# The Fourier branch's linear map on half the positions, gated there, in an encoder block on one core

## The chip, the cores and the metric

The kernel runs on one core of a Trainium2 chip. A core has a matrix engine (TensorE, PE in the profile, with its weight loads as PEld), a vector engine (VectorE, DVE), an activation engine (ScalarE, ACT), a general one (GpSimd, POOL), a queue that mostly issues transfers (SyncE, SP), and 16 DMA engines. They run side by side, each in its own order of instructions, and wait for each other by semaphores. The metric is the device time of one execution in microseconds (us).

## What is computed

One layer of an encoder on two sequences with shared weights: 1024 positions ("sample") and 256 ("prompt"), each with 16 learned meta positions ahead, width 1024. The part that matters here:

```python
z = rms_norm(x) @ w_in                  # q | k | v | f (512) | gate logits attn (1024) | gate logits four (1024)
a  = bidirectional_gqa(q, k, v) @ w_attn_o
fo = fourier_mix(f) @ w_four_o          # real part of the 2-D DFT over positions and 128 group channels
merged = sigmoid(z_ga) * a + sigmoid(z_gf) * fo
x = x + merged @ w_out                  # then a SwiGLU with a second norm, and a final norm
```

The real part of such a transform has a symmetry: with E (cosine in both directions) and O (sine in both), the value at position l and channel k is E - O or E + O, and at the mirrored position L - l the sign in front of O changes. So E and O need to be known only for positions up to L/2, and channels up to 64.

## The kernel before

All is in float32; a product is made of three matmuls on float32r parts, high x high, high x low and low x high (`three`, the lines L218 to L220, so that most matmuls carry these lines whatever they compute). Parts are made by a cast on ACT (high) and a subtraction on DVE or POOL (low). SBUF is 48 equal slots, given out in the order of the program, the longest free first.

The 1280 output positions are three chunks of 512, 512 (sample) and 256 columns (prompt). The stages, in order:

- A: norms, transposed activations `hT[c]` of each chunk, and the Fourier channels f.
- B and C: `fourier`, `q_pass`, `kv_pass`. `fourier` makes E and O: for the prompt all 256 positions unfolded, for the sample 520 positions, copied a second time mirrored with ACT. They go to DRAM (`f_d`, by chunk). `weave` puts steps of a gate generator between the steps of these passes, a share of their cost. `gate_gen([0], ...)` makes the 16 units (128 columns each) of gate logits of chunk 0: weights loaded, split, 24 matmuls, the result copied by ACT and stored in DRAM.
- D: `attention`, a unit is a query tile (128) and a key head, four query heads to a unit. A step is one query head: scores S (six matmuls for the sample, L898, into one buffer of three banks), maximum on DVE (L903), exponential on ACT (L910), scaling by the reciprocal sum on DVE (L915). Between them run the transposes (L832) of the unit before, their casts (L834) and low parts (L835), and the products with the values (L852, L853). The order on PE, ACT and DVE is the program's. Gate units of chunks 1 and 2 fill PE: at two points of each step a `Filler` gets credit in nanoseconds and issues steps of the generator for it; what these need of other engines is put into `later` and released at the second point (the "slack" point).
- E: `merge([0])`, then `merge([1, 2])`: for each of 8 units of 128 output columns load the weights (`w_m`: 4 k tiles of attention, 4 of Fourier; `w_mb`, whose sums with the Fourier half DVE makes at L992 and L993), split them (ACT, POOL), load both gates, sigmoid of both on ACT, for each chunk 4 k tiles of matmuls for the attention and 4 for the Fourier half, then two products with the gates (L1036, L1037), a sum (L1038) and the parts for the output projection. `load_af` brings attention and Fourier rows of a chunk and splits them. Then `w_out`.
- F: the SwiGLU, from 940 us on.

The functions that the change touches, and what calls them:

Of the kernel before, what the change touches and what calls it, by code (L numbers as in the profile page):

```python
# [9 lines left out]
F32 = mybir.dt.float32  # L10
# [26 lines left out]
# pairs of token tiles of the SwiGLU's products: the first three with 384 columns, the others with 256  # L37
# [18 lines left out]
SLOT = 1056  # L56
N_SLOTS = 27
# [58 lines left out]
class Slot:  # L116
# [32 lines left out]

class Filler:  # L150
    """Steps of a generator on demand."""

    def __init__(self, gen):
        self.gen, self.debt, self.live = gen, 0.0, True

    def __call__(self, cost):
        self.debt += cost
        while self.live and self.debt > 0:
            try:
                self.debt -= next(self.gen)  # L160
            except StopIteration:
                self.live = False
# [11 lines left out]
class Kernel:  # L174
    def __init__(self, tc, nc, a, o, pools):
# [18 lines left out]
        self.f_d = [self.dram.tile([512, n], F32, name=f"f_d{i}") for i, n in enumerate(CH_N)]  # L194

# [17 lines left out]
    def three(self, out, pairs, first=True, last=True):  # L213
        """out += hi.hi + hi.lo + lo.hi over pairs of ((stationary hi, lo), (moving hi, lo))."""
# [7 lines left out]
    def rstd(self, ss, n, scale, eps, name):  # L222
        """(ss * scale + eps) ** -0.5 for n sums a partition."""
# [7 lines left out]
    def norm(self, x, out, g, rows=P, name=""):  # L231
        """out = x * rsqrt(mean(x^2) + eps) (* g) along the columns."""
# [16 lines left out]
    # hT of chunk c: k pairs a slot (c0, c1), three k a slot (c2 with the meta tokens behind)  # L249
# [22 lines left out]
    def transpose_pair(self, hs, t, off, ps, name, tag="tr"):  # L272
        """Two token tiles (slots, 1024 columns) into hT columns off .. off+256."""
# [12 lines left out]
    def gained(self, t, ks, lo, hi, pt):  # L286
        """hT columns lo .. hi of some k tiles from the transposed rows, times the gains of their features."""
# [134 lines left out]

    FILL = {"s": 640, "p": 400, "end": 640, "drain": 900}

    def gate_gen(self, chunks, lo_engine):
        """Gate logits of the chunks; while there is a self.later, what is not for TensorE is put into it."""
        nc, a, sl = self.nc, self.a, self.sl
        order = list(range(16))
# [55 lines left out]

    def fourier(self, ps):
        nc, a, sl = self.nc, self.a, self.sl
        # even and odd parts over positions n <-> L - n
# [26 lines left out]
        # channels: U[n, k] for every n tile, cos from the even part, sin from the odd part  # L514
# [34 lines left out]
        for j, m in enumerate((P, 9)):  # L549
            nc.gpsimd.dma_start(tp[j][:m, :1024], a["pos_p"][j, :m])  # L550
# [25 lines left out]
        def store(kind, p, st, dst, lo, hi, c):  # L576
            """Rows of the (E0, E1, O0, O1) tiles; row 0 of each group's odd tile is k = 64."""
            d = dst[:]
            if kind == "e":
                nc.sync.dma_start(d[p * P : (p + 1) * P, :], st[:, lo:hi])  # L580
            elif kind == "o":
                for r in (0, 64):
                    b = 256 + p * P + r
                    nc.sync.dma_start(d[b + 1 : b + 64, :], st[r + 1 : r + 64, lo:hi])
            else:
                nc.sync.dma_start(d[256:512, :].rearrange("(g r) t -> g r t", g=4)[:, 0, :], st[:4, lo:hi])

        # prompt: positions 16.. unfolded
        ms = [P, 9]
        for kind, p in kinds:  # L590
            rows = 4 if kind == "4" else P
            pf = ps.tile([P, 512], F32, tag="mm", name=f"fp{kind}{p}")
            tb = 512 if kind == "o" else 0
            self.three(
                pf[:rows, :256],
                [
                    (u_of(kind, p, up, j, m), (tp[j][:m, tb : tb + 256], tp[j][:m, tb + 256 : tb + 512]))
# [4 lines left out]
            nc.vector.tensor_copy(st[:rows, :256], pf[:rows, :256])  # L602
            store(kind, p, st, self.f_d[2], 0, 256, 2)
# [3 lines left out]
        # sample: positions l = 1..520, the others mirrored  # L607
# [9 lines left out]
        for i, (kind, p) in enumerate(kinds):  # L617
# [5 lines left out]
            for half in range(2):  # L623
# [9 lines left out]
                sgn = -1.0 if kind == "o" else 1.0  # L633
                if half == 0:
                    nc.vector.tensor_copy(st[:rows, 0:245], pf[:rows, 15:260])
                    nc.scalar.mul(st[:rows, 764:1024], pf[:rows, 259::-1], sgn)
                else:
                    nc.vector.tensor_copy(st[:rows, 245:505], pf[:rows, 0:260])
                    nc.scalar.mul(st[:rows, 505:764], pf[:rows, 258::-1], sgn)
                yield 1650  # L640
            for c in range(2):
                store(kind, p, st, self.f_d[c], c * 512, (c + 1) * 512, c)
# [57 lines left out]
    def kv_pass(self, ps):  # L700
# [3 lines left out]
        # kT[seq][head][version]: columns are keys, the meta keys behind the tokens  # L704
# [94 lines left out]

    def attention(self, ps, tiles, tag_s, tag_v):  # L800
        """Scores and softmax of a unit (a query tile, a key head) run between the second products of the
        unit before it; the order is the one of the program."""
# [12 lines left out]
        class Second:  # L815
            """P^T and its product with the values, a key tile at a time."""
# [53 lines left out]
        def turns(k):  # L870
            """The k-th of the two parts of a step's share of the waiting key tiles."""
# [9 lines left out]
        for i, (t, g) in enumerate(units):  # L881
# [55 lines left out]

    def load_af(self, c):
        """a^T (4 k tiles) and Fourier (4 k tiles) of chunk c, 1024 columns a slot."""
# [29 lines left out]
    def merge(self, chunks, then):  # L969
# [35 lines left out]
        if 0 not in chunks:  # L1005
            for c in chunks:
                run_all(self.load_af(c))
# [716 lines left out]
```

## Time and profile before

| | |
|---|---|
| median of 3 runs | 1741.12 us (1739.78 to 1742.13) |
| profiled execution, first to last instruction | 1737.8 us |
| PE busy | 1697.8 us, 9917 matmuls |
| DVE / ACT / POOL busy | 1140.9 / 720.6 / 239.6 us |
| granted PE clock | 0.997 |
| moved by DMA | 212 MB, 122 GB/s over the span |

The profile lists for each engine the time in which it had an instruction under way. Matmuls overlap (the next starts before the last has left the array), so PE can be "busy" all the time and still do more or less work in it; the distance from start to start is what a matmul costs in a dense row. Groups are named by line, engine, operation and by the program's names of what is written and read; behind the bar stand busy time, mean duration in ns and the idle time before them with what ended it.

### The profile page before, as it was taken

Reading aid. Unit: us, or ns where it says so; the run is one execution under the profiler, and the core shown is the slowest. Engines: PE = TensorE matmul, PEld = TensorE weight load, DVE = VectorE, ACT = ScalarE, POOL = GpSimd, SP = SyncE. Lnnn points to the kernel's source line nnn. Section 1 sums busy time; section 2 is a strip of 40 time slices with the busy share of each in tenths; the row PEclk is TensorE's granted clock in tenths of the full one; section 3 lists DMA queues with packets and bytes.
Section 4 is the critical chain, followed back from the end, with each engine's and each line's share of the span. In section 5 each row is a group of like instructions: output and inputs, shape, how many; then the busy total and the mean of one; then the engine's idle time right before and its main releaser. Section 6 shows DMA issues by size and latency. Waiting matters only on the chain.

```text
span 1737.8 us, 25952 instructions
## 1 busy us (share of the span) xinstructions
PE 1697.8 (98%) x9917; PEld 1511.1 (87%) x9917; DVE 1140.9 (66%) x2084; ACT 720.6 (41%) x1391; POOL 239.6 (14%) x239
## 2 busy tenths in 40 slices
PE   7999999999999999999999999999999999999997
PEld 6888879878888888788879999999999998888886
DVE  5424544568777776963379766676666668765685
ACT  6323333456666666531355322222222234444444
POOL 3001333210100103423343000000000000000002
PEclk9999999999999999999999999999999999999999
DMA  5144331322222229735451222222232237553434
GB/s 190 63 149 162 116 116 55 122 74 67 70 61 59 61 79 352 250 119 170 145 182 64 85 82 95 90 96 89 94 98 84 71 126 255 198 182 101 159 97 153
DMA packets 100292, 212.06 MB, mean 122 GB/s; under 512 B 10373, under 2 KB 46877, under 8 KB 100168
## 3 DMA queue, kind: packets, MB, share of 16 engines
q1 hardware_dynamic: 90952, 192.98, 33.2%
q10 hardware_dynamic: 7824, 12.53, 2.0%
q0 software_dynamic: 1392, 4.90, 0.9%
q8 instruction: 78, 1.28, 0.3%
q14 instruction: 46, 0.38, 0.1%
HBM read 151.05 MB, written 59.31 MB: 121 GB/s over the span
## 4 chain that ended last, share of the span: by engine, by line
PE 67%; DVE 7%; DMA 3%; issue 3%; ACT 1%; POOL 1%; SPq 0%; POOLq 0%; DVEq 0%; ACTq 0%
PE i L218 9%; PE i L220 9%; PE i L219 9%; PE o L220 5%; PE o L219 5%; PE o L218 5%; PE S L898 4%; PE pt L832 4%; PE g L218 2%; PE pv L852 2%; PE g L219 2%; PE g L220 2%; PE pv L853 2%; PE wo L220 2%; PE wo L219 2%
## 5 line engine op out<-in xcount | busy, mean ns | idle before, releaser
L1227 ACT CAST w<-wi 128x512 fp32r<-128x512 f32 x168 | 104.0, 621 | 274.0 <-PE i L220 218.0
L218 PE MATMUL i<-A,w 128*128 128x384 f32 x616 | 208.4, 338 | 3.0 <-ACT w L1227 2.6
L220 PE MATMUL i<-A,w 128*128 128x384 f32 x616 | 208.1, 338 | 2.3 <-POOL w L1229 2.3
L219 PE MATMUL i<-A,w 128*128 128x384 f32 x616 | 207.9, 338 | 0.0
L218 PE MATMUL i<-Ah,w 128*128 128x256 f32 x616 | 173.0, 281 | 1.6 <-DVE sc L1283 1.5
L220 PE MATMUL i<-Ah,w 128*128 128x256 f32 x616 | 173.2, 281 | 0.0
L219 PE MATMUL i<-Al,w 128*128 128x256 f32 x616 | 172.9, 281 | 0.0
L834 ACT CAST pT<-pt 128x512 fp32r<-128x512 f32 x156 | 90.7, 582 | 97.1 <-PE pt L832 94.3
L835 DVE TENSOR_TENSOR pT<-pt,pT 128x512 fp32r<-128x512 f32 x156 | 106.9, 686 | 34.2 <-ACT pT L834 33.0
L1229 DVE TENSOR_TENSOR w<-wi,w 128x512 fp32r<-128x512 f32 x154 | 105.3, 685 | 28.7 <-ACT w L1227 28.3
L903 DVE TENSOR_REDUCE sm<-S 128x1 f32<-128x1040 f32 (+1 forms) x80 | 86.5, 1082 | 50.7 <-PE S L898 47.4
L218 PEld LDWEIGHTS i<-A,w 128*128 128x128 f32 x616 | 116.5, 189 | 3.6 <-ACT w L1227 2.9
L220 PEld LDWEIGHTS i<-A,w 128*128 128x128 f32 x616 | 116.4, 189 | 3.2 <-POOL w L1229 3.2
L218 PEld LDWEIGHTS i<-Ah,w 128*128 128x128 f32 x616 | 116.0, 188 | 2.2 <-DVE sc L1283 1.7
L219 PEld LDWEIGHTS i<-A,w 128*128 128x128 f32 x616 | 116.3, 189 | 0.0
L219 PEld LDWEIGHTS i<-Al,w 128*128 128x128 f32 x616 | 116.2, 189 | 0.0
L220 PEld LDWEIGHTS i<-Ah,w 128*128 128x128 f32 x616 | 116.0, 188 | 0.0
L227 POOL TENSOR_SCALAR fin0r<-fin0ss 128x1 f32<-128x1 f32 x1 | 0.8, 788 | 755.8 <-ACT X L235 755.8
L910 ACT ACTIVATE p<-S,sm 128x1040 f32<-128x1040 f32 (+1 forms) x80 | 80.2, 1003 | 33.6 <-DVE sm L903 27.0
L832 PE MATMUL pt<-ident,p 128*128 128x128 f32 (+1 forms) x624 | 93.4, 272 | 0.0
L220 PE MATMUL o<-wfo,act 128*128 128x512 f32 (+1 forms) x212 | 82.1, 388 | 2.1 <-DVE act L1361 2.1
L219 PE MATMUL o<-wfo,act 128*128 128x512 f32 (+1 forms) x212 | 81.9, 386 | 0.0
(745 smaller groups left out, 4475.9 us busy)
## 6 DMA issues: line engine op xcount, KB each, us to landing
wi<-w_fi SPq DMA_DIRECT2D x48, 512.0 KB
wg<-w_g SPq DMA_DIRECT2D x32, 512.0 KB
act_d<-sc SPq DMA_DIRECT2D x77, 192.0 KB
act<-act_d SPq DMA_DIRECT2D x37, 320.0 KB
wfo<-w_fo SPq DMA_DIRECT2D x21, 512.0 KB
X<-act_d SPq DMA_DIRECT2D x31, 320.0 KB
act_d<-sc SPq DMA_DIRECT2D x77, 128.0 KB
gate<-gs ACTq DMA_DIRECT2D x32, 256.0 KB
```

The source lines that it names most:

```text
L218: mm(out, sh, mh, start=first and i == 0, stop=False)
L219: mm(out, sh, ml, start=False, stop=False)
L220: mm(out, slo, mh, start=False, stop=last and i == n - 1)
L832: nc.tensor.transpose(pt[:rows, h * P : (h + 1) * P], me.ps4[h][:, col : col + rows], self.ident[:])
L834: nc.scalar.copy(pT[:rows, :512], pt[:rows, :])
L835: nc.vector.tensor_tensor(pT[:rows, 512:1024], pt[:rows, :], f32(pT[:rows, :512]), op=ALU.subtract)
L852: nc.tensor.matmul(me.pv[:], vst, pT[:rows, :512], start=j == 0, stop=False)
L898: nc.tensor.matmul(S[:, base + lo : base + hi], hq, self.kT[seq][g][v][:, lo:hi], start=v == 0, stop=v == 1)
L903: nc.vector.tensor_reduce(nb, S[:, base : base + L], axis=AX.X, op=ALU.max, negate=True)
L910: self.last_exp = nc.scalar.activation(p, S[:, base : base + L], AF.Exp, bias=nb, accum_out=total)
L1227: nc.scalar.copy(w[:, :512], src)
L1229: eng.tensor_tensor(w[:, 512:1024], src, f32(w[:, :512]), op=ALU.subtract)
```

## The change

1. `fourier` computes E and O only for positions 1 to 520 of the sample and 1 to 136 of the prompt, side by side in one table of 656 columns in DRAM; the k = 64 rows have a place of their own. The mirrored copies go.
2. The gate logits 8 to 15 (of the Fourier branch) are made for all three chunks in stages B and C, and their sigmoid is taken there before they are stored; logits 0 to 7 of chunk 0 come first in the same filler, with a share of 1.1 instead of 0.6. The attention's filler has logits 0 to 7 of chunks 1 and 2 and then a new generator, `fourier_out`; its credit is 480 and 300 ns a point instead of 640 and 400.
3. `fourier_out` applies `w_four_o` to E and O (two halves of 328 positions, two accumulators each), forms sum and difference on POOL (the second in reversed order), multiplies by the gates on POOL and stores the gated term (`fo_d`) in the order of output positions.
4. `merge` has 4 k tiles instead of 8. It loads one gate and the gated term, and keeps the split weights of the first merge (chunk 0) for the second; the low parts of these weights are made by DVE, not POOL.

The diff without the comments that it drops:

```diff
-    FILL = {"s": 640, "p": 400, "end": 640, "drain": 900}
+    FILL = {"s": 480, "p": 300, "end": 640, "drain": 900}
...
+    def __call__(self, cost, later=None):
         self.debt += cost
+        if self.held and later:
+            return
+        self.held = False
...
-            nc.scalar.copy(st[:, :n], pg[:, :n])
+            if u < 8:
+                nc.scalar.copy(st[:, :n], pg[:, :n])
+            else:
+                nc.scalar.activation(st[:, :n], pg[:, :n], AF.Sigmoid)
...
+    def fourier_out(self):
+        nc, a, sl = self.nc, self.a, self.sl
+        self.free_hT(self.hT[1])
+        self.free_hT(self.hT[2])
...
+        def need(i):
+            w = raws.pop(i)
+            vec = nc.vector.tensor_tensor
+            vec(w[:, :256], w[:, :256], w[:, 512:768], op=ALU.add)
+            vec(w[:, 256:512], w[:, 768:1024], w[:, 256:512], op=ALU.subtract)
+            u = units[i] = sl.get("wmf2", F32R)
+            nc.scalar.copy(u[:, :512], w[:, :512])
+            vec(u[:, 512:1024], w[:, :512], f32(u[:, :512]), op=ALU.subtract)
...
+        def part(r):
+            nc.scalar.copy(h[:, :NL], r[:, :NL])
+            nc.gpsimd.tensor_tensor(l[:, :NL], r[:, :NL], f32(h[:, :NL]), op=ALU.subtract)
...
+        def tail(r, t, n, lo):
+            for b in (0, 32, 64):
+                nc.scalar.copy(t[b : b + 4, :n], r[b : b + 4, :n])
+            x = slice(lo, lo + 4)
+            nc.gpsimd.tensor_tensor(t[x, :n], r[x, :n], f32(t[x, :n]), op=ALU.subtract)
...
+        do(lambda: need(0))
+        for r, t, _, n, lo in tails:
+            do(lambda r=r, t=t, n=n, lo=lo: tail(r, t, n, lo))
+        for r in raw:
+            do(lambda r=r: part(r))
+        yield 1500
+        for i in range(8):
+            for half in range(2):
...
+                    if odd == 0:
+                        nc.tensor.matmul(
+                            pm[:, :HL], y64[:68, i * P : (i + 1) * P], x64[:68, c], start=True, stop=False
+                        )
+                    for k in range(2 * odd, 2 * odd + 2):
...
+                        self.three(pm[:, :HL], [(w, (fh[k][:, c], fl[k][:, c]))], odd == 1 and k == 2, k % 2 == 1)
+                        yield 3 * HL / 2.2
+                if half == 0:
+                    do(lambda i=i: (need(i + 1), load(i + 2), load_gates(i + 1)))
+                def out(i=i, half=half, pp=pp):
+                    nc.scalar.copy(st[:, :HL], pp[0][:, :HL])
+                    nc.scalar.copy(st[:, 512 : 512 + HL], pp[1][:, :HL])
...
+                    for l, n, L, b, t0 in spans:
+                        nc.gpsimd.tensor_tensor(d, x[:, skip:], y[:, skip:], op=ALU.add)
+                        nc.gpsimd.tensor_tensor(d, d, g[:, t : t + n - skip], op=ALU.mult)
+                        nc.sync.dma_start(self.fo_d[i][:, t : t + n - skip], d)
+                        nc.gpsimd.tensor_tensor(d, x[:, n - 1 :: -1], y[:, n - 1 :: -1], op=ALU.subtract)
+                        nc.gpsimd.tensor_tensor(d, d, g[:, t : t + n], op=ALU.mult)
+                        nc.sync.dma_start(self.fo_d[i][:, t : t + n], d)
...
+                do(out)
+                yield None
...
     def merge(self, chunks, then):
+        first = 0 in chunks
...
-            nc.sync.dma_start(wa[:, :1024], a["w_m"][i])
-            nc.sync.dma_start(wb[:, :512], a["w_mb"][i])
+            if first:
+                nc.sync.dma_start(wa[:, :512], a["w_ma"][i])
...
-                nc.sync.dma_start(gt[:, n : 2 * n], self.gates[8 + i][c][:])
+                nc.sync.dma_start(gt[:, n : 2 * n], self.fo_d[i][:, 512 * c : 512 * c + n])
...
-            nc.vector.tensor_tensor(wa[:, 512:768], wa[:, 512:768], wb[:, :256], op=ALU.add)
-            nc.vector.tensor_tensor(wa[:, 768:1024], wb[:, 256:512], wa[:, 768:1024], op=ALU.subtract)
-            hl = self.split(wa, 1024, "wm", None, "t")
+            if first:
+                nc.scalar.copy(hl[:, :512], wa[:, :512])
+                nc.vector.tensor_tensor(hl[:, 512:1024], wa[:, :512], f32(hl[:, :512]), op=ALU.subtract)
...
-            weave(ahead(self.fourier(ps), QSTART, q_pass), gates, 0.6)
-            weave(ahead(q_pass, KVSTART, kv_pass), gates, 0.62)
-            weave(kv_pass, gates, 0.6)
+            weave(ahead(self.fourier(ps), QSTART, q_pass), gates, 1.1)
+            weave(ahead(q_pass, KVSTART, kv_pass), gates, 1.1)
+            weave(kv_pass, gates, 1.1)
...
-            gates = Filler(self.gate_gen([1, 2], self.nc.gpsimd))
+            gates = Filler(chain(self.gate_gen(range(8), [1, 2], self.nc.gpsimd), self.fourier_out()))
```

More of the change, by code (lines that the diff above doesn't have):

```diff
@@ L632, in fourier @@
                 )
[L633 to L639, printed above, removed]
+                (nc.scalar.copy if half else nc.vector.tensor_copy)(st[:rows, b : b + 260], pf[:rows, :260])
                 yield 1650
-            for c in range(2):
-                store(kind, p, st, self.f_d[c], c * 512, (c + 1) * 512, c)
+            store(kind, p, st, 0, NLS)
             sl.put(st)
@@ L943, in load_af @@
         out = self.af[c] = []
-        pieces = [(srcs, j) for srcs in (self.a_d[c], [self.f_d[c]]) for j in range(4 // per)]
+        pieces = [(self.a_d[c], j) for j in range(4 // per)]
         loaded = {}
@@ L1004, in merge @@
         af = self.af
-        if 0 not in chunks:
+        if not first:
             for c in chunks:
-                run_all(self.load_af(c))
+                if c not in af:
+                    run_all(self.load_af(c))
         for c in chunks:
@@ L1042, in merge @@
                 sl.put(gt)
-            sl.put(wh, wl)
+            if not first:
+                sl.put(hl)
         for c in chunks:
@@ L1525, in build @@
             self.mm = ps, "g"
-            gates = self.gate_gen([0], self.nc.vector)
+            four = self.gate_gen(range(8, 16), [0, 1, 2], self.nc.vector)
+            gates = chain(self.gate_gen(range(8), [0], self.nc.vector), four)
             q_pass, kv_pass = self.q_pass(ps), self.kv_pass(ps)
@@ L1556, in build @@
                         later.popleft()()
-                    gates(self.FILL[kind] + more)
+                    gates(self.FILL[kind] + more, later)
                 while later:
```

164 lines of the change are left out of this document (116 added, 48 removed).

## The prediction

> **What bounds the kernel now.** I read the page first, its busy times and the chain that ended last, to see which engine's work is the time.
>
> ```profile
> span 1737.8 us, 25952 instructions
> ...
> PE 1697.8 (98%) x9917; PEld 1511.1 (87%) x9917; DVE 1140.9 (66%) x2084; ACT 720.6 (41%) x1391; POOL 239.6 (14%) x239
> ...
> PE 67%; DVE 7%; DMA 3%; issue 3%; ACT 1%; POOL 1%; SPq 0%; POOLq 0%; DVEq 0%; ACTq 0%
> ```
>
> PE is busy 1697.8 of 1737.8 us and holds most of the chain, so a matmul less shortens the kernel by its pitch, as long as nothing else makes PE wait. The span is 3.3 us below the median of the runs, 1741.1; I make the sum as a difference and add it to the median.
>
> Then the windows, by stage. Columns: length, PE, PEld, DVE, ACT and POOL busy (instructions), clock, DMA share, GB/s.
>
> ```profile
> 375.00:660.00 285.00, 283.82 (x1743) 243.11 (x1743) 219.61 (x327) 180.87 (x326) 30.19 (x23) 1.00 0.24 73
> ...
> 670.00:715.00 45.00, 45.00 (x200) 36.76 (x200) 37.65 (x45) 24.14 (x28) 20.47 (x8) 1.00 0.93 343
> 715.00:760.00 45.00, 40.99 (x223) 34.37 (x223) 36.93 (x55) 21.72 (x30) 12.62 (x5) 1.00 0.57 193
> ```
>
> The sample attention (375 to 660) keeps PE full, but DVE is at 219.6 of 285, 77%. The merge (670 to 787) has DVE at 84% and 82%, DMA at 93% in its first part, and 4.0 us of PE idle in the second. Those two stages decide whether saved matmuls become saved time.
>
> Pitch of a matmul is the distance of starts, not the duration. The order of time on PE:
>
> ```profile
> 663.89 0.39 PE L218 MATMUL g<-hT1h,wgh 128*128 128x512 f32 x1
> ...
> 668.08 0.28 PE L218 MATMUL g<-hT2h,wgh 128*128 128x256 f32 x1
> ...
> 670.91 0.40 PE L218 MATMUL m<-wmh 128*128 128x512 f32 x1
> ...
> 787.55 0.39 PE L218 MATMUL wo<-woh,wmh 128*128 128x512 f32 x1
> ```
>
> 18 matmuls of 512 columns start from 663.89 to 668.08: 0.233 us each. 24 of 256 columns from there to 670.91: 0.118. A straight line between them gives 328 columns 0.150. The merge lasts from 670.91 to 787.55, 116.6 us.
>
> **The change, part by part: PE's work.** The merge loses its Fourier half: 8 units x 4 k tiles x 3 products = 96 matmuls for each chunk, 96 x (0.233 + 0.233 + 0.118) = **-56.0**. The new step (`fourier_out`) has 8 units x 2 halves x (12 + 1) matmuls of 328 columns, 208 x 0.150 = **+31.2**. The columns are fewer because only the 656 positions up to the mirror are mapped, instead of 1280.
>
> In the Trainium skill, "TensorE: Matmul & The Clock Gate", section "Back-to-back issue gap" gives N/2.4 + 2.5 ns: 139 ns for 328 columns, 216 for 512 and 109 for 256. By it these two terms would be -51.9 + 29.0 = -22.9 instead of -24.8; the trace's pitches are 8% longer, and the sum goes by the trace.
>
> ```profile
> 100.70 0.39 PE L531 MATMUL uep<-T,fep 128*128 128x65 f32 x2
> 100.92 0.39 PE L532 MATMUL uop<-T,fop 128*128 128x64 f32 x2
> ...
> 106.32 0.27 PE L220 MATMUL fpe<-tabp,ue 128*128 128x256 f32 x1
> 106.53 0.38 PE L218 MATMUL fpe<-tabp,ue 9*128 9x256 f32 x1
> 106.75 0.27 PE L219 MATMUL fpe<-tabp,ue 9*128 9x256 f32 x1
> ```
>
> Of the 13 matmuls the extra one (the k = 64 channel) contracts 68 rows. Going from 128 rows to 9 costs: the gaps are 0.21 and 0.22 instead of 0.118, so 0.19 on the way in, and as much on the way out. Bounds 0 and 16 x 0.38 = 6.1; 68 rows fill over half the array, so nearer to 128 than to 9: **+1**. The prompt's positions shrink from 256 to 136 columns, 30 matmuls. The nearest narrow rows: two matmuls of 65 columns in 0.22, so 0.11 each. If that is a floor, 30 x (0.110 - 0.118) = -0.2; if it grows with the columns, 0.23 each, +3.4. I take **0**, as the weights are 128 wide in both. Work in all: **-23.8**.
>
> The gate logits 8 to 15 of chunks 1 and 2 move from the attention to the passes before it: 8 x 24 x (0.233 + 0.118) = 67 us of the same matmuls, no net change. So the attention's filler falls from 16 x 24 x 0.351 = 134.8 to 67.4 + 31.2 = 98.6, and by the code's own costs the credit (93.3) just covers it (91.5), starting the new step after some 41 of the 64 sample steps and ending two half-steps before the drain's end.
>
> **What the waits cost.** A sample step now:
>
> ```profile
> 507.11 1.11 PE L898 MATMUL S<-kT,qT 128*128 128x264 f32 x6
> 508.26 1.24 DVE L903 TENSOR_REDUCE sm<-S 128x1 f32<-128x1040 f32 x1 [0.56 <-PE S L898]
> 509.58 1.13 ACT L910 ACTIVATE p<-S,sm 128x1040 f32<-128x1040 f32 x1 [0.30 <-DVE sm L903]
> 511.27 0.99 PE L898 MATMUL S<-kT,qT 128*128 128x264 f32 x5
> ```
>
> There is one S buffer: scores, maximum, exponential, next scores form a loop. It closes at 510.71, and PE comes back at 511.27: slack 0.56. The credit falls from 1280 to 960 a step, 0.35 us of PE, so 0.2 is left. Uneven fillers will eat it now and then: **+1.5** (0 to 6, 0.1 us for each of 64 steps).
>
> ```profile
> L443 ACT CAST wgh<-wg 128x512 fp32r<-128x512 f32 x60 | 36.1, 622 | 27.2 <-DMA wg<-w_g 17.4 <-PE f L219 4.8 <-DVE qs L775 1.5
> L202 ACT CAST woh<-wo 128x1024 fp32r<-128x1024 f32 x16 | 16.6, 1048 | 58.6 <-PE wo L220 45.9 <-DMA wo<-w_out 7.9 <-DVE ml L1041 2.5
> L834 ACT CAST pT<-pt 16x512 fp32r<-16x512 f32 x20 | 11.3, 564 | 3.7 <-PE pt L832 3.7
> ```
>
> Start of the new step: one slack point releases, on ACT in order, six copies of four rows (three of 656 columns, three of 1024; 16 rows cost as much as 128 by L834), four casts of 656 columns and one of 512. By L443 and L202, 0.75 for 656: 7 x 0.75 + 3 x 1.05 + 0.62 = 9.0 us, with the next exponential behind them, and Pool's low parts behind those. Of a step of 4.16 (511.27 - 507.11) ACT has 4.16 - 1.13 - 2.25 x 0.56 = 1.8 free, so PE would stand 7; less if they overlap, 2; with weights not landed, 14: **+7**.
>
> ```profile
> L835 DVE TENSOR_TENSOR pT<-pt,pT 128x512 fp32r<-128x512 f32 x99 | 68.0, 687 | 18.0 <-ACT pT L834 17.1
> L903 DVE TENSOR_REDUCE sm<-S 128x1 f32<-128x1040 f32 x49 | 60.9, 1242 | 22.5 <-PE S L898 22.5
> ...
> L915 DVE TENSOR_SCALAR p<-p,sm 128x1040 f32<-128x1040 f32 x50 | 38.1, 762 | 1.9
> ```
>
> Each later unit puts on DVE, at a slack point, two sums of 256 columns (some 0.4 each, from 0.69 for 512) and a low part of 512 with an ACT cast between: 0.4 + 0.4 + 0.62 + 0.69 = 2.1 us in front of the next maximum, which waits for PE only 0.56. DVE's own part of a step with two key tiles is 1.24 + 0.76 + 2 x 0.69 = 3.4, of 4.16 now and 3.8 after. Seven units: nothing if the gaps take it, 7 x 2.1 = 15 if none does; **+7**, one a unit, as half of each gap is used up.
>
> Pool now gets four operations a half on SBUF data. What this does to DVE:
>
> ```profile
> 331.41 0.36 DVE L915 TENSOR_SCALAR p<-p,sm 128x272 f32<-128x272 f32 x1
> ...
> 345.79 1.28 POOL L444 TENSOR_TENSOR wgl<-wg,wgh 128x512 fp32r<-128x512 f32 x1 [9.96 <-ACT wgh L443]
> 346.21 1.02 DVE L915 TENSOR_SCALAR p<-p,sm 128x272 f32<-128x272 f32 x1
> ...
> 694.24 2.83 POOL L203 TENSOR_TENSOR wmh<-wm,wmh 128x1024 fp32r<-128x1024 f32 x1 [2.58 <-ACT wmh L202]
> 694.72 2.63 DVE L992 TENSOR_TENSOR wm<-wm,wmb 128x256 f32<-128x256 f32 x1
> ```
>
> The scaling of 272 columns takes 0.36 alone and 1.02 beside Pool, ending just after Pool's operation; a sum of 256 columns takes 2.63. So Pool's work is not free for DVE: in the attention it adds, in the merge it goes away, since the merge no longer splits weights on Pool nor sums them on DVE. The merge's work before is 2 x 56.0 = 112, so of 116.6 us 4.6 were waits; I give back **-3** (-4.6 if all goes; +6 if the loads, three of 256 KB each 2.8 us of PE in chunk 0 = 281 GB/s plus the attention rows, run into the 343 GB/s shown at 93%, or w_out's first weights, with half the merge's unit to hide behind, come late).
>
> Rest: at the attention's end before, gate matmuls (663.89 to 670.91) covered the sum and split of the first attention rows; now the filler has run out: **+3** (0 to 7, by those 7.0 us). Into the upper end goes SP's queue: it issues 48 stores of gated terms, each behind Pool's product, and the merge's loads stand behind the last of them; a half keeps Pool for some four operations of 0.85 (1.28 for 512 columns by L444, above), 3.4 us. The prompt's steps lose filler they partly idled in: **+1** (0 to 4). Before the attention more filler covers waits: **-1** (-2.5 to +3). Two more table loads on ACT stay in those bounds. Waits in all: 1.5 + 7 + 7 - 3 + 3 + 1 - 1 = +15.5.
>
> **Sum:** -23.8 + 15.5 = -8.3; 1741.1 - 8.3 = **1732.8**.
>
> **The rivals.** *Pool and DVE hold up the scores (ends slower).* Mechanism: in the last 22 sample steps Pool is busy half the time, and each scaling and each unit's sums wait for its operations, so DVE and not PE paces them. A wait of half an operation of 0.85 at each of 22 scalings is 9 us, and the units' sums cost their full 15. Then -23.8 + 15.5 + 9 + 8 = +8.7, **1750**. It decides from about 8 us beyond my sum on. For it: the rows above; against it: the scaling is followed by a low part that waits for ACT anyway (idle 18.0 us before L835), so part of the wait is taken up. The Trainium skill, "SBUF — State Buffer", section "SBUF: two separate sides", calls the pair of ports that the two engines share an exclusive lock, held for the whole instruction; the two stretched rows agree with it.
>
> *Nothing left (same).* The start at 12 and the units at 10 us instead of 7 and 7: -23.8 + 23.5, **1741**. For it: the whole release sits in front of an exponential.
>
> *The saving comes through.* Start and units 5 together, the merge without waits: -23.8 + 0.9 + 4 = -19, **1722**. For it: 77% DVE leaves 65 us free in the attention.
>
> **How the numbers follow.** My sum's case 0.45 and the full saving 0.10 are faster; the tie 0.17; Pool and DVE 0.28. A difference below 0.2% (3.5 us) is about what a measurement can't tell from none. So faster 0.55, same 0.17, slower 0.28. The likeliest case alone spans 1726 to 1737; with the tie and the slower rival, and the full saving at the low end, the range is 1722 to 1750.
>
> **What would show it.** The merge, first m to first wo, should take 56 plus a few us; the attention should lose 36 us of filler and get back some 17, with one gap of PE of several us before the first `fo` matmul, ended by ACT or Pool, and seven short ones at S; the scaling of 1040 columns should have a mean above 0.76 in the last steps. Wrong would be: a gap elsewhere, matmuls of 328 columns at another pitch than 0.150, or a merge paced by DMA.

## The result, and the profile after

The changed kernel takes 1811.68 us (median of 4 runs, 1810.79 to 1813.71) against 1740.80 for the kernel before on the same chip: ratio 1.0411, 95% interval 1.0396 to 1.0426. The prediction said 1732.8 us and a range that ended at 1750: wrong in sign, and outside the range.

The page of the changed kernel, the lines that answer to the prediction's first fence, and the granted clock in 40 slices:

```profile
span 1809.0 us, 25962 instructions
...
PE 1704.2 (94%) x9837; PEld 1510.2 (83%) x9837; DVE 1101.4 (61%) x2050; ACT 713.1 (39%) x1409; POOL 247.7 (14%) x311
...
PEclk9999999999999899889999999999999999999999
...
PE 52%; DVE 4%; ACT 2%; issue 2%; POOL 2%; DMA 1%; SPq 0%; POOLq 0%; ACTq 0%; DVEq 0%
```

There are 80 matmuls fewer, and yet PE is "busy" 6 us longer: part of them ran at a lower clock (the 8s in slices 14, 17 and 18, of 45 us each: 588 to 633 and 724 to 814). The span is 71.2 us longer.

To see where, I cut both executions at the exponentials, one for each of the 80 score steps (16 of the prompt, then 64 of the sample). Before, in the order of time, the 1st, 57th, 61st and last:

```profile
317.42 0.49 ACT L910 ACTIVATE p<-S,sm 128x272 f32<-128x272 f32 x1
...
535.78 1.13 ACT L910 ACTIVATE p<-S,sm 128x1040 f32<-128x1040 f32 x1 [0.25 <-DVE sm L903]
...
553.71 1.13 ACT L910 ACTIVATE p<-S,sm 128x1040 f32<-128x1040 f32 x1 [0.31 <-DVE sm L903]
...
639.06 1.13 ACT L910 ACTIVATE p<-S,sm 128x1040 f32<-128x1040 f32 x1 [0.31 <-DVE sm L903]
```

and the same four after the change:

```profile
382.73 0.49 ACT L914 ACTIVATE p<-S,sm 128x272 f32<-128x272 f32 x1
...
590.01 1.13 ACT L914 ACTIVATE p<-S,sm 128x1040 f32<-128x1040 f32 x1 [0.25 <-DVE sm L907]
...
624.32 1.13 ACT L914 ACTIVATE p<-S,sm 128x1040 f32<-128x1040 f32 x1
...
745.61 1.13 ACT L914 ACTIVATE p<-S,sm 128x1040 f32<-128x1040 f32 x1 [0.25 <-DVE sm L907]
```

With the merge's bounds (670.91 and 787.55 before, 782.77 and 857.49 after) this gives, in us:

| stretch | before | after | difference | predicted |
|---|---|---|---|---|
| up to the first exponential | 317.4 | 382.7 | +65.3 | +66.4 |
| steps 1 to 57 (filler: gates) | 218.4 | 207.3 | -11.1 | |
| steps 57 to 61 (after: the new step starts) | 17.9 | 34.3 | +16.4 | |
| steps 61 to 80 (after: the halves of the new step) | 85.3 | 121.3 | +36.0 | |
| last exponential to the merge | 31.9 | 37.2 | +5.3 | |
| attention, the four together | 353.5 | 400.0 | +46.5 | -15.7 |
| merge | 116.6 | 74.7 | -41.9 | -59 |
| the rest | 950.3 | 951.5 | +1.2 | 0 |

The predicted column is the prediction's own terms, put where they fall: 67.4 of gate matmuls less 1 before the attention; in the attention -67.4 + 31.2 + 1 of work and 19.5 of waits; in the merge -56.0 - 3.

The loss lies in two stretches of 20 and 120 us, and in a merge that gave less. Who PE waited for, over the whole execution (us in total, times, longest):

```profile
PE fo L1027 <- ACT fst L1044: 20.0, 9, 3.7
PE fo L1027 <- ACT p L1044: 13.5, 6, 4.1
PE fo L1027 <- POOL y L1008: 10.2, 1, 10.2
PE S L902 <- ACT p L914: 9.3, 16, 1.6
PE m L232 <- ACT mh L1136: 6.8, 1, 6.8
```

The third row is the start of the new step: the prediction had one gap of PE of several us before the first `fo` matmul, ended by ACT or Pool. The first two rows were not in the prediction at all: before every half but the first, PE stands at the half's first matmul (L1027) until ACT has copied the accumulators of the half before (L1044), 15 times, 33.5 us. (`p` and `fst` are names of the same kind of slot.)

One such handing over, and the start of the half after it, in the order of time (some lines left out):

```profile
654.07 1.14 ACT L914 ACTIVATE p<-S,sm 128x1040 f32<-128x1040 f32 x1
...
654.56 0.40 PE L857 MATMUL pv<-pT,v 128*128 128x512 f32 x1
...
655.18 0.58 ACT L838 CAST pT<-pt 128x512 fp32r<-128x512 f32 x1
655.80 0.69 DVE L839 TENSOR_TENSOR pT<-pt,pT 128x512 fp32r<-128x512 f32 x1 [0.63 <-ACT pT L838]
...
656.74 0.42 DVE L975 TENSOR_TENSOR wmf<-wmf 128x256 f32<-128x256 f32 x1
657.24 0.62 ACT L977 CAST pT<-wmf 128x512 fp32r<-128x512 f32 x1 [1.47 <-issue]
...
657.76 0.43 ACT L1044 COPY fst<-fo 128x328 f32<-128x328 f32 x1
...
658.24 0.64 PE L1027 MATMUL fo<-pT,y 68*128 68x328 f32 x1 [3.28 <-ACT fst L1044]
...
658.68 0.47 PE L232 MATMUL fo<-fh,wmf 128*128 128x328 f32 x1
658.95 0.47 PE L233 MATMUL fo<-pT,wmf 128*128 128x328 f32 x1
...
669.60 0.42 PE L1027 MATMUL fo<-pT,y 68*128 68x328 f32 x1 [1.60 <-ACT p L1044]
...
670.01 0.31 PE L233 MATMUL fo<-pT,pT 128*128 128x328 f32 x1
670.16 0.32 PE L234 MATMUL fo<-fh,pT 128*128 128x328 f32 x1
```

A half fills both banks of PSUM (where the sums of matmuls are kept) that the kernel gives the filler, an accumulator in each. Its two copies are released at the slack point, behind the exponential, a cast, and after a unit's first half also behind the weight cast, which waits for DVE's sums (the 1.47 is put down to issue, but the sum before it ended at 657.16). PE is in order: the next score matmuls stand behind the waiting L1027. When it comes back its matmuls start 0.27 us apart (658.68, 658.95), not the 0.150 of the prediction, which the half after a gap of 1.60 shows (670.01, 670.16). The granted clock from 658.04 to 661.45 is 0.50. So the gap of 3.28 us costs its idle time and then 3.4 us of half speed.

The Trainium skill, "TensorE: Matmul & The Clock Gate", section "HAM oscillation — how this bites in real kernels", warns of idle gaps of TensorE above some 3.4 us, after which it restarts at half its clock. The trace agrees on the half clock and not on the bound: before L1027 six gaps of 3.24 to 4.07 us and one of 2.23 (763.75) each came with a stretch of 3.4 us or more at 0.50 that began within 1 us of their end, and the five of 1.20 to 1.64 did not. The length alone does not decide it: in e17 below a gap of 1.83 us was followed by half clock (668.30), and in e5 one of 2.93 was not (711.76).

The windows of the changed kernel (length, PE, PEld, DVE, ACT, POOL busy, clock, DMA share, GB/s):

```profile
380.00:595.00 215.00, 206.61 (x1237) 171.75 (x1236) 162.50 (x267) 131.23 (x254) 18.67 (x15) 1.00 0.25 74
595.00:613.00 18.00, 6.65 (x39) 5.00 (x37) 8.17 (x13) 12.12 (x19) 5.36 (x4) 0.83 0.25 75
613.00:640.00 27.00, 20.17 (x92) 16.24 (x90) 13.26 (x22) 11.55 (x21) 8.97 (x8) 0.80 0.21 66
640.00:700.00 60.00, 45.61 (x257) 37.74 (x257) 38.17 (x59) 30.15 (x59) 17.55 (x32) 0.94 0.34 100
```

With gates as filler the clock is 1.00; from the start of the new step it is 0.80 to 0.94, and no engine is busy more than 76% of the time (PE, 45.61 of 60): no engine is the bound by its work alone; they wait for each other in turn.

### The profile page after: what moved, and what is told of

Same layout as the page of the kernel before. It is cut to its first block, busy times and chain, and to the rows that moved or that the text cites. A ratio compares the mean times of both kernels' runs of the same rounds, so it can differ in the third digit from the quotient of the medians.

```text
span 1809.0 us, 25962 instructions
## 1 busy us (share of the span) xinstructions
PE 1704.2 (94%) x9837; PEld 1510.2 (83%) x9837; DVE 1101.4 (61%) x2050; ACT 713.1 (39%) x1409; POOL 247.7 (14%) x311
## 2 busy tenths in 40 slices
DMA packets 106780, 209.33 MB, mean 116 GB/s; under 512 B 12221, under 2 KB 54361, under 8 KB 106656
## 4 chain that ended last, share of the span: by engine, by line
PE 52%; DVE 4%; ACT 2%; issue 2%; POOL 2%; DMA 1%; SPq 0%; POOLq 0%; ACTq 0%; DVEq 0%
PE i L234 9%; PE i L232 9%; PE i L233 9%; PE o L234 5%; PE o L233 4%; PE o L232 4%; PE wo L233 1%; PE wo L232 1%; PE wo L234 1%; PE m L232 1%; PE m L233 1%; PE m L234 1%; PE S L902 1%; DVE sm L907 1%; PE pt L836 1%
## 5 line engine op out<-in xcount | busy, mean ns | idle before, releaser
L234 PEld LDWEIGHTS i<-A,w 128*128 128x128 f32 x616 | 116.6, 189 | 3.1 <-POOL w L1372 3.0
```

What stands on the lines that cost most here:

```text
L234: mm(out, slo, mh, start=False, stop=last and i == n - 1)
```

## The experiments

Theory A: the handing over of the two PSUM banks makes PE run dry. B: GpSimd's work holds up VectorE. C: the weight sums on VectorE do. D, formed on the way: SP's queue, or SBUF slots that are still being stored. Times are compared with 1811.7 unless another run is named. e1, e5 and e12 were run four times, the others once; repeated runs of one kernel here lie within 0.3% (5 us). Cut as in the table above, the attention's last stretches and the merge were (us):

| run | time | steps 57-61 | 61-80 | to the merge | merge |
|---|---|---|---|---|---|
| before | 1740.8 | 17.9 | 85.3 | 31.9 | 116.6 |
| the change | 1811.7 | 34.3 | 121.3 | 37.2 | 74.7 |
| e1 each accumulator apart, handed on late | 1809.8 | 34.3 | 117.4 | 35.3 | 78.3 |
| e2 copies first | 1790.6 | 34.8 | 106.8 | 31.2 | 72.7 |
| e3 filler waits one point more | 1791.4 | 34.5 | 103.0 | 33.2 | 76.5 |
| e4 tails cast in two | 1808.8 | 31.2 | 121.8 | 39.0 | 73.2 |
| e5 each accumulator apart, at once | 1792.8 | 34.6 | 113.7 | 25.8 | 74.6 |
| e7 = e5 without GpSimd's work | 1770.2 | 35.6 | 99.5 | 23.5 | 67.5 |
| e8 = e5 without weight sums | 1780.5 | 33.6 | 103.5 | 26.2 | 73.0 |
| e11 = e5 without both | 1765.5 | 35.2 | 96.7 | 24.4 | 66.0 |
| e9 stores on GpSimd's queue | 1818.0 | 34.8 | 126.7 | 40.6 | 70.7 |
| e10 = e5 + e4 + e9 | 1804.5 | 31.9 | 123.4 | 29.1 | 73.8 |
| e13 lighter merge loads | 1804.9 | 34.6 | 121.3 | 39.3 | 65.1 |
| e15 start under gate products | 1800.9 | 20.9 | 120.0 | 37.6 | 73.7 |
| e17 = e5 + slots given back late | 1781.1 | 34.6 | 105.0 | 27.7 | 70.9 |
| e18 = e17 + e15 | 1775.5 | 20.9 | 105.6 | 26.1 | 72.4 |

**e1, e2, e3: the handing over of the banks.** e1 copies and releases each accumulator by itself:

```diff
     for odd in range(2):
+        while pend[odd]:
+            yield None
...
+        pend[odd] = True
+        do(lambda ...: copy(odd, pm, slots))
```

> Each accumulator of the new step is copied out and released by itself, and the next group starts only when its own bank was copied; the order puts the copies ahead of the weight sums. Theory A (both banks of the filler are held by one half, so the next half's first matmul waits for ACT's copies, 33.5 us in 15 waits, and the idle PE then runs at a lower clock): these waits fall under 8 us, the granted clock between 640 and 760 us goes from 0.89-0.94 to above 0.97, the time falls by 30 to 50 us, to 1760 to 1780. Theory B (Pool's operations hold up DVE and with it the scores): no matmul or Pool operation is less, so the time changes by under 10 us. Theory C (the weight sums of each unit on DVE stand before the maximum): they are still there, 7 x 2 us; the time changes by under 15 us.

Measured: 1809.78 (ratio 1.0400, 1.0383 to 1.0417). A's expectation failed. PE's waits in e1, from 590 to 790:

```profile
PE fo L1038 <- ACT fst L1030: 19.7, 12, 3.6
...
PE fo L232 <- ACT fst L1030: 8.7, 10, 1.6
```

With two shorter rows for the same copies (1.6 and 0.5) that is 30.5 us instead of 33.5, in 24 waits instead of 15. The edit was no good test: a copy was only put in line when the filler was called again, a point late, and PE went on at the very point at which the copies were released.

e2 moves the copies ahead of the next unit's weight sums and cast:

```diff
-                if half == 0:
-                    do(lambda i=i: (need(i + 1), load(i + 2), load_gates(i + 1)))
...
                 do(out)
+                if half == 0:
+                    do(lambda i=i: (need(i + 1), load(i + 2), load_gates(i + 1)))
```

> Only the order in which a half's work is released: the copies out of the accumulators ahead of the next unit's weight sums and cast. Theory A: the waits after first halves (3.2 to 4.4 us each, seven of them) come down to those after second halves (1.0 to 2.0), 7 x 2.2 = 15 us, with clock some 20: about 1792. Theory B: no change (within 4 us). Theory C: no change, since DVE's sums stay in front of the maximum.

Measured: 1790.59, 21 us less; the 15 waits shrank to 19.0 us in all, and the granted clock from 640 to 760 rose from 0.91 to 0.99. e3 keeps the old order, but the filler goes on one point after the copies' release:

```diff
-        if self.held and later:
+        if self.held:
+            if not later:
+                self.held = False
             return
```

> After a half the filler waits one release point more before it starts the next half, so PE has the next scores and transposes between. Theory A: the 15 waits of 33.5 us in front of a half's first matmul fall under 10 us and the clock recovers; but fewer halves fit into the attention and some run behind it without cover (up to 5 halves, some 4 us each by Pool): 1770 to 1795. Theory B: 1805 to 1815. Theory C: as B.

Measured: 1791.39, 20 us less. The waits of L1027 for the copies fell to 8.0 us, those of the scores for the exponential grew from 9.3 to 11.3 (12 times). Two edits that touch nothing but the place of the copies against the work beside them each gave 20 us back, where B and C had next to nothing; so that much of A is shown.

**e5, e7, e8, e11: what else holds the halves.** e5 does what e1 meant to: the copy is put in line right behind the accumulator's last matmul. e7, e8 and e11 leave work out of e5.

```diff
+                        if k % 2 == 1:
+                            pend[odd] = True
+                            do(lambda ...: copy(odd, pm, slots))
+                            if odd:
+                                do(out)
+                                if half == 0:
+                                    do(lambda i=i: (need(i + 1), load(i + 2), load_gates(i + 1)))
                         yield 3 * HL / 2.2
```

> The change, but each of a half's two accumulators is handed on alone: its copy is put in line behind its last matmul at once (not at the filler's next turn), it stands ahead of the next unit's weight sums and cast, and the half's second bank is filled while the first is copied. Theory A (the handing on of the two banks lets TensorE run dry and its clock fall): the waits of the first matmul of an accumulator for ScalarE, 33.5 us in all with the change, fall under 12, the phase from the last gate to the merge goes from 188 us to 140-155, the time to 1765-1780. Theory B (GpSimd's sums and gating hold up VectorE): no better than with the copies first, 1790. Theory C (the weight sums on VectorE hold the halves): 1790 too, since they stay.

> As the run with accumulators handed on alone, but GpSimd's sum, difference and two gatings of each half are left out: what ScalarE copied goes out as it is. Theory B: at least 15 us under that run. Theory A: within 6 us of it, since GpSimd works beside everything else.

> As the run with accumulators handed on alone, but units 1 to 7 use unit 0's weights: their three VectorE passes over the weights and ScalarE's cast are left out. Theory C: at least 15 us under that run. Theory A: 5 to 10 us under it (7 x 0.62 us of ScalarE and 7 x 1.5 us of VectorE that lie between the score steps).

> Accumulators handed on alone, GpSimd's work on the halves left out, and unit 0's weights used for all units: of the new step only its products, two copies a half and its stores are left. If the costs of GpSimd (22.6 us) and of the weight sums (12.3 us) add, 1758. If they are one and the same wait (the score steps' turn of VectorE), about 1768. In both, the last 19 score steps, which took 121 us with the change and 85 before, take under 97.

Measured: e5 1792.77 (ratio 1.0296, 1.0276 to 1.0316), e7 1770.15, e8 1780.46, e11 1765.47. In e5 PE's waits for the copies are 6.0 us, as A had it, but the time fell by 19 us and not by 32 to 47, to about the 1790 that B and C had, and the clock from 640 to 760 is still 0.91: A was only part of it. e7 is 22.6 us under e5, for which A had at most 6 and B at least 15; e8 12.3, between what A and C had (it also holds fewer slots, as units 1 to 7 take none for their split weights). Both together save 27.3 and not 34.9, so they partly are one wait, as the expectation's second case had it. What was the price of GpSimd's work? ACT's waits in e5, from 600 to 765:

```profile
ACT pT L838 <- DMA fo_d<-fsd: 5.4, 1, 5.4
...
ACT p L914 <- DMA fo_d<-fsd: 3.7, 1, 3.7
...
ACT ao L862 <- DMA fo_d<-fsd: 2.7, 1, 2.7
...
ACT fsd L914 <- DMA fo_d<-fsd: 2.3, 1, 2.3
```

An exponential, a cast of P^T and an attention result wait here for *stores of the gated term*: they were given a slot that GpSimd had just filled and that was not yet stored. SBUF's slots go round, longest free first, and few are free.

**e9, e10: SP's queue.**

```diff
-                        nc.sync.dma_start(self.fo_d[i][:, t : t + n - skip], d)
+                        nc.gpsimd.dma_start(self.fo_d[i][:, t : t + n - skip], d)
```

> The change with one thing else: the gated halves are stored from GpSimd's DMA queue and no longer from SP's, where they waited 58 us for GpSimd with the weight loads, the attention's stores and the merge's first loads behind them. Theory D (that queue sets when weights come and slots are free): at least 15 us under the change, 1795 or less. Theory A (the two PSUM banks): 3 to 8 us under it (the merge's first product waits 6.8 us less or so, the halves as long as before).

> All the mendings inside the attention together: accumulators handed on alone, stores on GpSimd's queue, the tails cast in two copies and not six. Against the run with accumulators handed on alone (1792.8): theory D 15 to 20 us less, 1773-1778; theory A 5 to 11 us less, 1782-1788. Neither brings it to the kernel before.

Measured: 1817.95 and 1804.46; 9 and 16 us above the worst that A or D gave. The queue form of D falls, and the stores are better where they were. GpSimd issues them itself (e9, groups of instructions from 600 to 770):

```profile
L1059 POOL DMA_DIRECT2D fo_d<-fsd x12 | 7.7, 640 | 0.0
L1067 POOL DMA_DIRECT2D fo_d<-fsd x12 | 6.5, 541 | 0.0
```

0.59 us each, 48 of them; that they lengthen the half's way through GpSimd, and so the time its slots are held, is the likely reason and was not tried by itself. The merge did get shorter (70.7 against 74.7): there the stores had stood ahead of its loads.

**e17: the slots.** The two slots of a half go back two halves later; nothing else differs from e5.

```diff
-                    sl.put(st, sd)
+                    busy.append((st, sd))
+                    if len(busy) > 2:
+                        sl.put(*busy.popleft())
```

> As the run with accumulators handed on alone (1792.8), but the two slots of a half go back two halves later, when they have long been stored, so that no exponential, cast or copy is given one that is still being stored. Theory D in its narrower form (ScalarE's 16 us of waits for stores of fo_d and for GpSimd): 10 to 16 us under that run, 1777 to 1783. Theory B (GpSimd's work beside VectorE's, or the time it takes itself): within 4 us of 1792.8.

Measured: 1781.13, 11.6 us under e5, and from 600 to 765 ACT waits for no store of `fo_d` any more. The narrower D holds: half of what GpSimd's work cost was that others got its slots too early. The other 11 us were not taken apart; in e5 the low part of the weights took 1.23 us on DVE where it takes 0.69 otherwise, which speaks for some of B.

**e4, e15, e18: the start.** e4 casts the two tails in one copy of 68 rows each instead of three of 4 rows. e15 frees room early (the last gate unit takes its 256 columns first) and spreads loads and casts over that unit's 24 matmuls of 512 columns:

```diff
+                    if n == 120:
+                        self.free_hT(self.hT[2])
+                    if n == 120 or n >= 122:
+                        next(four)
```

> The twelve rows of the k = 64 channel are cast with one copy of 68 rows instead of three of four rows each, so two copies less for each of the two tables: ACT's burst loses 2 x 0.75 + 2 x 1.05 = 3.6 us. If that burst is what PE waits for in front of the first new matmul (10.2 us), the wait falls to 6 to 7 and the time by 4 to 6 us (the clock with it). If it is the landing of the loads (DVE waits 1.9 us for the weights), the time changes by under 1.5 us.

> The change, but the last gate unit takes its 256 columns first, so that room comes free early, and the loads and casts of the new step are spread over the 24 products of 512 columns that remain. If the start is dear because nothing covers its loads and casts: score steps 56 to 60 take 20 to 25 us and not 34.3, the time is 9 to 14 us under the change. If the casts themselves on ScalarE are the price (they stand between exponentials either way): 0 to 5 us under it.

> The same with the loads and casts of the new step spread over the last gate unit as well. If the mendings add, 8 to 12 us under the run with the late slots. Still slower than the kernel before in every theory.

Measured: e4 1808.80, 2.9 us less (expected 4 to 6), which is within the spread of single runs; in the profile steps 57 to 61 are 3.1 us shorter. e15 1800.93, 10.7 us less, inside 9 to 14: steps 57 to 61 fall from 34.3 to 20.9, while the four steps before them, in which the casts now lie, rise from 16.9 to 23.5. So the start itself gained 6.8 us; the rest lies in later stretches, 1.3 at most in each, and can be the spread. e18 1775.45, 5.7 us under e17, where 8 to 12 was expected: the mendings do not quite add. All three together bring the change from 1811.7 to 1775.5, half of the loss.

**e13, e14: the merge.** Both leave out the part of the attention's product that comes from the low parts of the values (the expectation calls it a half of the heads and 5.2 MB; it is this half of what the merge reads of the attention, and the bytes moved fell by 2.6 MB, from 209.33 to 206.71), e13 from the change, e14 from the kernel before.

```diff
-        pieces = [(self.a_d[c], j) for j in range(4 // per)]
+        pieces = [(self.a_d[c][:1], j) for j in range(4 // per)]
```

> The change, but the merge reads one of the two halves of the attention's heads and not both (5.2 MB less to load, no sum on VectorE); what it computes is short of that half. If the merge with half the products is paced by its loads (they ran at a share of 1.04 for 35 of its 75 us): merge 62 to 66 us, the whole 9 to 13 us under the change. If it is paced by its products and their waits: merge within 3 us of 74.7.

> The same taken from the kernel before, as a control: its merge of 116.6 us has the loads at a share of 1.03 for 19 us only and TensorE busy for 112.6. If products pace it: merge 113 to 117 us, the whole 0 to 4 us under the kernel before.

Measured: the merge of the change fell from 74.7 to 65.1, that of the kernel before went from 116.6 to 117.2. The totals fell by 6.8, short of the 9 to 13 expected (the merge began 2 us later after the last exponential), and 3.1. So the shortened merge waits for its loads, and for VectorE's sum that each pair of them needs and that the edit leaves out too; the long one did not. Windows of the merge, the first 35 us and the rest, in the change:

```profile
782.77:818.00 35.23, 26.68 (x97) 19.72 (x97) 24.10 (x35) 15.65 (x26) 3.21 (x4) 0.85 0.93 322
818.00:857.49 39.49, 36.76 (x192) 31.63 (x192) 30.09 (x49) 17.28 (x33) 2.39 (x1) 0.91 0.48 159
```

and in the kernel before, its first 19 us and the rest:

```profile
670.91:690.00 19.09, 19.09 (x85) 15.54 (x84) 12.95 (x22) 11.03 (x14) 6.79 (x4) 1.00 1.02 388
690.00:787.55 97.55, 93.54 (x495) 79.09 (x494) 82.38 (x108) 41.73 (x55) 32.58 (x13) 1.00 0.56 195
```

Before, DMA was at 1.02 too, but PE had 93.5 us of products left behind it. Now a third of the merge's matmuls (97 of 289) take 35 of its 75 us, beside DMA at 0.93 and a clock of 0.85. PE's longest wait there, 6.8 us, ends with the cast of a unit's weights, whose load was still under way:

```profile
789.00 0.46 SPq L1120 DMA_DIRECT2D wm<-w_ma  x1
...
794.20 0.62 ACT L1136 CAST mh<-wm 128x512 fp32r<-128x512 f32 x1 [9.95 <-DMA wm<-w_ma]
...
794.87 0.80 PE L232 MATMUL m<-wm,mh 128*128 128x512 f32 x1 [6.77 <-ACT mh L1136]
```

PE had stopped at 788.10, before that load was issued: on SP's queue it stood behind the last stores of gated terms (785.63, 786.04) and of attention results (786.52), and from 782 to 788 DMA was at 0.40. So the loads' start has a share in this beside their rate, and e13 does not tell the two apart.

**e12, e16: the same step in another place.** In e12 the gates stand as before the change, and the new step follows the attention with four banks; VectorE makes sums and differences, GpSimd only multiplies, the sigmoids come after the last exponential, and the tails are cast as in e4. e16 loads one unit earlier.

```diff
-    FILL = {"s": 480, "p": 300, "end": 640, "drain": 900}
+    FILL = {"s": 640, "p": 400, "end": 640, "drain": 900}
...
-            gates = Filler(chain(self.gate_gen(range(8), [1, 2], ...), self.fourier_out()))
+            gates = Filler(self.gate_gen([*range(8, 16), *range(8)], [1, 2], ...))
...
+            for n, _ in enumerate(fo):
...
             run_all(m0)
```

> The same sums in another place: the gates stand in the order of the kernel before (filler of the attention again, at 640 and 400), and the Fourier product of 520 and 136 positions, its gating and the one-term merge follow the attention, with four PSUM banks; VectorE makes the sums and differences, GpSimd only multiplies, the sigmoids come after the last exponential. If the place beside the scores is what costs (A, B, C and D alike): attention 355 us as before, 38 to 50 us for the product, 62 to 70 for the merge, together 1725 to 1748. If the step itself is dear anywhere (ScalarE, VectorE and GpSimd as long as its products): 60 us or more for the product, 1755 or more.

> The version with the product behind the attention, its weights, gates and the merge's first operands loaded one unit earlier. If it was held by late loads: 1738 to 1743. If by the transfers' rate (a share of 0.81 to 1.03 from the product's start to the middle of the merge): within 3 us of 1747.3.

Measured: e12 1747.32 (ratio 1.0045, 1.0028 to 1.0062); e16 1751.42, outside both of its cases. In e12 attention, product, and the merge in two windows:

```profile
314.50:668.25 353.75, 349.57 (x2121) 297.59 (x2121) 257.40 (x404) 213.54 (x407) 49.22 (x37) 1.00 0.26 78
668.25:717.82 49.57, 38.40 (x211) 35.10 (x209) 27.12 (x65) 22.47 (x42) 25.71 (x43) 0.86 0.86 277
717.82:765.00 47.18, 34.84 (x126) 25.66 (x127) 32.89 (x48) 23.25 (x38) 4.22 (x6) 0.82 0.93 326
765.00:792.93 27.93, 27.93 (x165) 24.65 (x164) 21.75 (x39) 11.96 (x24) 2.39 (x1) 1.00 0.34 111
```

The attention is the kernel before's again (each interval of its score steps agrees within 0.1 us), and e12 stands 7.8 us above its own kernel before (1739.5), the change 70.9 above its own. So 63 of the 71 us go with the place of the gates and of the new step, together with what e12 altered beside it (the banks, VectorE's sums). What remains: product and merge take 49.6 + 75.1 = 124.7 us where the merge alone took 116.6, though they have 25 us less of matmuls (62 to 70 were expected of the merge); for 97 of these 125 us DMA is at 0.86 to 0.93. In e16 the product took 59.4 (PE waits 12.6 us there for the copies) and the merge 72.3: product and merge together 131.6 against 124.7. Earlier loads did not shorten the wait, which fits a limit by the transfers' rate and not by their start; that it is the rate was not tried by itself. No version of the change beats the kernel before.

## Why the prediction was wrong

The prediction had PE's work right and failed in what PE waits for. In the attention it left out the handing over of the two banks and the slots still being stored, and put the start too low; in the merge it took 3 us of waits off, where a stage with half the products had to wait for its loads. Term by term:

- **PE's work, -23.8.** Count and full-speed pitch hold: 208 matmuls, 0.150 us apart where PE did not stand before (670.01 to 670.16). The matmul of 68 rows takes 0.11 more (669.60 to 669.86, the next start); 16 of them make 1.8, where the sum has +1. The step "matmuls of 328 columns at 0.150" still failed where it followed a gap (0.27).
- **The handing over of the banks: missing from the sum.** The prediction priced what the new step puts on ACT, DVE and POOL, and not what PE waits for between two halves with two accumulators in two banks. 33.5 us of waits; e2 and e3 give 21 and 20 us for moving it.
- **Start, +7 (2 to 14).** 16.4 measured. The burst of ACT was sized well (10.2 us of wait against 9.0 of casts), but I let the step's slack absorb part of it, and the half clock afterwards was not in the sum. With cover (e15) 6.8 us come back there.
- **Weight sums, +7 (0 to 15).** e8: 12.3 us in e5; in the range, not at its middle.
- **Pool and DVE hold up the scores (the slower rival, +9 and +8).** The mechanism named, scaling stretched by Pool's operations, is small: the scaling's mean from 600 to 770 is 785 ns against 762. Pool's work was dear by another way, slots still being stored (e17, 11.6 us). The rival had the sign right and the place wrong; "a mean above 0.76" was true and no proof.
- **Narrower slack, +1.5 (0 to 6).** The credit falls by 0.35 us in 40 sample steps, and by some 0.2 in the 16 of the prompt: 17 us by this estimate; steps 1 to 57 gained 11.1, so 6 were lost, at the end of the range.
- **Merge, -3 (-4.6 to +6).** 56.0 us of matmuls went, 41.9 came: the term is +14.1. The prediction named the loads at 281 GB/s and bounded them by +6; measured are 322 GB/s at a share of 0.93 over 35 us (e13 against e14). The saving of matmuls took away the cover of the same loads; I judged the stage by its average PE time. How much of it is their rate and how much their late start behind SP's stores stays open.
- **End of the attention +3, before it -1:** 5.3, inside its bounds; -2.1 (65.3 less 67.4), inside too.

The misses: attention 46.5 + 15.7 = 62.2, merge 17.1, the small ones 0.1; with the -8.3 that was forecast they give the 71.2 of the span. Of the attention's 62, the pieces shown by a run of their own are about 20 (banks), 7 (start), 12 (slots) and 12 (weight sums). They overlap, and even e11, which has hardly more than the products, needs 35.2 us for steps 57 to 61 and 96.7 for 61 to 80 where the kernel before needs 17.9 and 85.3; the 11 us of the last 19 steps stay open.

## What to carry to other kernels

Filler under a latency loop must never make the in-order engine wait: count its accumulators against its banks, and ask who empties a bank, what stands ahead of that copy, and what is queued behind the matmul that waits. A gap there can be paid twice: in the changed kernel those of 2.2 us and more were followed by 3.4 us or more of half clock. And when a stage's products are halved, its loads are not: compare what is left of the products with the time in which that stage's DMA share is 1, and not with the stage's average.

## What was not expected of the hardware

- On one core, idle gaps of PE of 2.2 to 4.1 us were followed by stretches of 3.4 us or more at half clock, in which matmuls of 328 columns started 0.27 us apart instead of 0.15; they took the mean clock of whole phases to 0.80-0.94.
- A DMA issue from GpSimd's queue takes 0.54 to 0.64 us of GpSimd (24 of them, 14.2 us from 600 to 770, in e9).
- A cast of 4 rows of 1024 columns takes ACT 1.04 us (the change), one of 68 rows the same 1.04 (e12).
